# Two PSUM pools of a hybrid encoder block, opened in the other order

## The chip, the cores and the metric

The kernel runs on one core of a Trainium2 chip. The metric is the device time of one execution in microseconds (us), as the median of several runs. Before the change it is 1249.9 us, the median of three runs from 1248.79 to 1251.98. A difference of 0.3% (3.7 us) is about the least that a measurement of this kernel can tell from no change.

## What is computed

One layer of an encoder for 256 tokens of width 2048, all in float32:

```
n = RMSNorm(h)
[GDN inputs | HGRN2 inputs] = n @ W_in
y_A = gated DeltaNet group (8 heads of 128)
y_B = HGRN2 group (8 heads of 128: gate, chunkwise recurrence, gated RMSNorm)
h = h + concat(y_A, y_B) @ W_out
h = h + relu(RMSNorm(h) @ W1)^2 @ W2
out = RMSNorm(h)
```

The change concerns the border between the last two HGRN2 heads and the product with W_out, a 256 x 2048 by 2048 x 2048 product.

## The kernel before

**Products.** A float32 operand is split in two float32r parts, `hi` (a cast on ScalarE, ACT, line 120) and `lo` (a subtraction on VectorE, DVE, line 121). Weights come in tiles of 128 x 2048 floats (`w`, 1 MB, three buffers), which SyncE (SP) loads in order. Each tile is split in two halves of 1024 columns into three buffers of `hi` and three of `lo`. So the cast of one half has to wait until TensorE (PE) has read the half three before it.

**Stages.** The input projection and the sixteen heads ("mixers") are software-pipelined: while the weights of head n+1 are multiplied (lines 331, 332 and 358), head n is mixed. Heads 0 to 7 are GDN, heads 8 to 15 HGRN2. After the input projection's last matmul, the mixing of heads 14 and 15 is left. Then comes the output projection (line 845): two passes (`nh` = 0, 1) of 16 blocks `k`, one for each head's 128 columns of y. A block is 12 matmuls of 512 columns: 4 with `hi` and 2 with `lo` for each of two halves of the tokens. A pass adds into four banks: `acc` for the first pass and `accb` for the second. The MLP follows (lines 874 to 876).

**The end of a mixer** (`hgrn_mix`). Its matmuls come in three groups. The names are those of their tiles:

- `pd` and `pa` (lines 693 to 708): the scores in the chunks. DVE masks and adds them up (711, 715), POOL spreads them (718) and ACT copies the rest (721 to 725) into `A`.
- `poh` (727 to 729): the head's output from `A`. ACT and DVE norm it (479 to 483).
- `pt` (487): its transpose. ACT and DVE (491, 492) write it to `yTa` (heads 0 to 11) or `yTb` (heads 12 to 15), which the output projection reads: block k reads head k.

Ahead of `pd` stands a chain of small steps on ACT, DVE and POOL (lines 639 to 682).

**Banks.** PSUM has eight banks of 2 KB a partition, and each tile here is one. `psM` holds the mixers' four (two `mx`, two `sv`). `psP` holds the input projection's four: two `acc` of `project`, two `tok` of `project_tokens`, which `tokens_out` (line 367, ACT) reads last. Both pools close at `mctx.close()`. Then `psA` (the `acc` above) and `psB` (`accb`) open, with four banks each. A pool takes the lowest banks free, so before the change `psA` takes those of `psM` and `psB` those of `psP`:

```python
    mctx.close()
    psA = ctx.enter_context(tc.tile_pool(name="psA", bufs=4, space=PSUM))
    psB = ctx.enter_context(tc.tile_pool(name="psB", bufs=4, space=PSUM))
    ...
    for nh in range(2):
        acc = (acc_a, acc_b)[nh]
        accs = [acc() for _ in range(4)]
```

**Order.** Each engine works through its instructions in the order in which they stand. That order comes from a scheduler, which lays the instructions out by its own estimate of when each could run. A matmul into a bank that a pool has taken over waits for the last reader of what was there.

Of the kernel before, what the change touches and what calls it, by code (L numbers as in the profile page):

```python
# [12 lines left out]
PSUM = bass.MemoryType.PSUM  # L13
# [62 lines left out]
def hybrid_block(ctx: ExitStack, tc: tile.TileContext, x, xt, w_in, w_ab, params, w_out, w_ff1, w_ff2,  # L76
# [19 lines left out]
    yTa = ypool.tile([P, NYA, 2 * T], F32R, tag="yT", name="yTa")  # L96
    mctx = ExitStack()
    mp = mctx.enter_context(tc.tile_pool(name="mp", bufs=1))
    psM = mctx.enter_context(tc.tile_pool(name="psM", bufs=MXB, space=PSUM))
    psP = mctx.enter_context(tc.tile_pool(name="psP", bufs=2, space=PSUM))  # L100

    def wtile():
        return wpool.tile([P, 2048], F32, tag="w", name="w")
# [1079 lines left out]
```

## Time and profile before

| | |
|---|---|
| median of 3 runs | 1249.9 us |
| the profiled execution | 1249.3 us, of which its span 1247.6 us |
| PE busy | 97% of the span |
| DVE, ACT, POOL busy | 83%, 62%, 10% |
| weights read and the rest | 233.44 MB, 187 GB/s in the mean |
| granted PE clock | 0.985 in the mean |

Times in the profile are counted from the start of the span. A row of the timeline gives the start, the length, the engine, the line and the operation, with the tiles written and read. In square brackets stands how long the engine had been idle, and what ended that. A row of the windows gives for a stretch each engine's busy time with its count of instructions, and then the granted clock of PE, the DMA engines' busy share and GB/s. "PEld" is the loading of PE's stationary operand, which overlaps the matmuls.

### The profile page before, as it was taken

The numbers are of one execution on the slowest core, as the hardware profiler recorded it, in microseconds if no ns is written. First come the engines' busy times: TensorE is split into PE (matmuls) and PEld (weight loads), VectorE is DVE, ScalarE is ACT, GpSimd is POOL, SyncE is SP. The second block draws the span as 40 slices with busy tenths as digits, with TensorE's granted clock in tenths as the row PEclk, the third lists the DMA queues.
The fourth block names the chain that finished last, engine by engine and source line by source line (L and its number), as shares of the span: only waits on it lengthen the run. The fifth ranks groups of instructions, "written<-read, shape, count | busy, mean of one in ns | idle before, by whom it ended". The sixth has DMA issues, their size and how long they took to land.

```text
span 1247.6 us, 18180 instructions
## 1 busy us (share of the span) xinstructions
PE 1215.6 (97%) x6894; PEld 1013.8 (81%) x6894; DVE 1033.4 (83%) x1443; ACT 776.8 (62%) x1150; POOL 118.9 (10%) x177
## 2 busy tenths in 40 slices
PE   9999999997999959999999999999999999999997
PEld 7888888886888848888888888888888888888886
DVE  7888997786779854768898989898998888988887
ACT  7668666664768653646655656666666656656553
POOL 0132432153211110000000000000000000000000
PEclk9999999998999969999999999999999999999999
DMA  9456455552335525765465455554775555565461
GB/s 332 160 161 200 159 190 180 190 177 93 103 136 203 168 69 169 246 210 188 165 236 200 172 202 203 188 187 165 276 273 198 201 199 203 184 221 201 170 236 68
DMA packets 37143, 233.44 MB, mean 187 GB/s; under 512 B 4696, under 2 KB 5728, under 8 KB 10176
## 3 DMA queue, kind: packets, MB, share of 16 engines
q1 hardware_dynamic: 34848, 229.83, 52.7%
q0 software_dynamic: 1632, 1.72, 0.7%
q8 instruction: 54, 0.88, 0.3%
q10 hardware_dynamic: 576, 0.74, 0.2%
q14 instruction: 33, 0.27, 0.1%
HBM read 227.67 MB, written 4.60 MB: 186 GB/s over the span
## 4 chain that ended last, share of the span: by engine, by line
PE 92%; POOL 2%; issue 2%; DMA 2%; DVE 1%; ACT 1%; SPq 0%; POOLq 0%; DVEq 0%; ACTq 0%
PE acc L358 10%; PE acc L875 9%; PE acc L876 9%; PE acc L874 9%; PE accb L875 8%; PE accb L874 8%; PE accb L876 8%; PE acc L331 8%; PE acc L332 4%; PE acc L845 4%; PE accb L845 3%; PE accv L331 2%; PE accv L332 1%; POOL X L513 1%; PE acc L886 1%
## 5 line engine op out<-in xcount | busy, mean ns | idle before, releaser
L121 DVE TENSOR_TENSOR lo<-w,hi 128x1024 fp32r<-128x1024 f32 (+1 forms) x422 | 485.8, 1167 | 124.3 <-ACT hi L120 116.5
L120 ACT CAST hi<-w 128x1024 fp32r<-128x1024 f32 (+1 forms) x422 | 413.5, 993 | 240.7 <-PE acc L875 53.1
L331 PE MATMUL acc<-xT,hi 128*128 128x512 f32 x512 | 180.6, 399 | 1.7 <-ACT hi L120 1.7
L120 ACT CAST hi<-TT 128x1024 fp32r<-128x1024 f32 x88 | 92.0, 1052 | 77.9 <-issue 21.7
L332 PE MATMUL acc<-xT,lo 128*128 128x256 f32 x512 | 140.4, 285 | 0.0
L121 DVE TENSOR_TENSOR lo<-TT,hi 128x1024 fp32r<-128x1024 f32 x88 | 106.8, 1221 | 29.5 <-ACT hi L120 27.2
L358 PE MATMUL acc<-hi,xT 128*128 128x512 f32 x384 | 119.1, 398 | 0.0
L331 PEld LDWEIGHTS acc<-xT,hi 128*128 128x128 f32 x512 | 94.9, 189 | 21.6 <-ACT hi L120 2.2
L874 PE MATMUL acc<-hi,sets 128*128 128x512 f32 x260 | 101.4, 391 | 0.0
L875 PE MATMUL acc<-hi,sets 128*128 128x512 f32 x260 | 101.2, 390 | 0.0
L332 PEld LDWEIGHTS acc<-xT,lo 128*128 128x128 f32 x512 | 96.7, 190 | 4.5 <-DVE lo L121 1.2
L876 PE MATMUL acc<-lo,sets 128*128 128x512 f32 x260 | 95.9, 390 | 0.0
L874 PE MATMUL accb<-hi,sets 128*128 128x512 f32 x224 | 88.0, 393 | 0.0
L875 PE MATMUL accb<-hi,sets 128*128 128x512 f32 x224 | 87.3, 390 | 0.0
L358 PEld LDWEIGHTS acc<-hi,xT 128*128 128x128 f32 x384 | 71.9, 191 | 14.9
L876 PE MATMUL accb<-lo,sets 128*128 128x512 f32 x224 | 78.8, 392 | 0.0
L875 PE MATMUL acc<-hi,gs 128*128 128x512 f32 (+1 forms) x200 | 77.0, 385 | 0.0
L874 PE MATMUL acc<-hi,gs 128*128 128x512 f32 (+1 forms) x200 | 76.7, 385 | 0.0
L1014 POOL TENSOR_TENSOR fin<-fin,cst 128x1 f32<-128x1 f32 x2 | 1.1, 568 | 781.2 <-DVE fin L1013 781.2
L876 PE MATMUL acc<-lo,gs 128*128 128x512 f32 (+1 forms) x200 | 75.6, 385 | 0.0
L358 PE MATMUL acc<-lo,xT 128*128 128x512 f32 x192 | 73.5, 399 | 0.0
L875 PE MATMUL accb<-hi,gs 128*128 128x512 f32 x188 | 73.1, 389 | 0.0
(362 smaller groups left out, 2359.6 us busy)
## 6 DMA issues: line engine op xcount, KB each, us to landing
w<-in_w_ff_dram SPq DMA_DIRECT2D x128, 1024.0 KB, 5.0
w<-in_w_in_dram SPq DMA_DIRECT2D x61, 1024.0 KB, 5.0
w<-in_w_out_dram SPq DMA_DIRECT2D x16, 1024.0 KB, 5.0
w<-in_w_in_dram SPq DMA_DIRECT2D x12, 256.0 KB, 5.4
big<-in_xt_dram SPq DMA_DIRECT2D x8, 256.0 KB, 5.6
h<-in_x_dram SPq DMA_DIRECT2D x2, 1024.0 KB, 8.6
scr_h<-h SPq DMA_DIRECT2D x4, 512.0 KB, 7.3
tail<-scr_h SPq DMA_DIRECT2D x2, 1024.0 KB, 6.0
```

The source lines that it names most:

```text
L120: ACT.copy(hi, w)
L121: eng.tensor_tensor(out=lo, in0=w, in1=hi.bitcast(F32), op=ALU.subtract)
L331: PE.matmul(accs[g], lhsT=hi[:, kk, g, :], rhs=xT[:, k, :], start=(k == 0), stop=False)
L332: PE.matmul(accs[g][:, T:], lhsT=lo[:, kk, g, :], rhs=xT[:, k, 0:T], start=False, stop=(k == KT - 1))
L358: PE.matmul(accs[hf], lhsT=xT[:, k, a + hf * P:a + hf * P + P], rhs=ww[:, cs], start=(k == 0 and a == 0 and ww is hi), stop=(k == KT - 1 a ...
L513: POOL.tensor_tensor(out=X[:, j + 1:, 0:ncol], in0=X[:, j + 1:, 0:ncol], in1=t3, op=ALU.subtract)
L845: PE.matmul(accs[2 * hf + c], lhsT=st, rhs=ww[:, c * 512:(c + 1) * 512], start=(k == 0 and a == 0 and ww is hi), stop=(k == 2 * NH - 1 and ...
L874: PE.matmul(dst, lhsT=ah, rhs=bh, start=start, stop=False)
L875: PE.matmul(dst, lhsT=al, rhs=bh, start=False, stop=False)
L876: PE.matmul(dst, lhsT=ah, rhs=bl, start=False, stop=stop)
L886: PE.transpose(pt[:, c * P:(c + 1) * P], src[:, c * P:(c + 1) * P], ident)
L1014: POOL.tensor_tensor(out=r, in0=r, in1=C("nhalf"), op=ALU.pow)
```

## The change

`psP` is opened ahead of `psM`. So the lower four banks are now the input projection's, and `psA`, which the output projection's first pass adds into, takes those. `psB` takes the mixers'.

```diff
     mp = mctx.enter_context(tc.tile_pool(name="mp", bufs=1))
+    psP = mctx.enter_context(tc.tile_pool(name="psP", bufs=2, space=PSUM))
     psM = mctx.enter_context(tc.tile_pool(name="psM", bufs=MXB, space=PSUM))
-    psP = mctx.enter_context(tc.tile_pool(name="psP", bufs=2, space=PSUM))
```

No instruction is added or taken away. The order of POOL and SP stays as it was. That of PE, ACT and DVE is changed only between the end of the input projection and the end of the output projection's first pass.

On PE, right after the last `pa` matmul of head 14, there stood the rest of head 14 and the whole of head 15, and then the first pass (lines with a minus are before, lines with a plus are now):

```order
 L708 MATMUL pa<-L 128x128
-L727 MATMUL poh<-ig,A 128x128
-L728 MATMUL poh<-ig,A 128x128
-L729 MATMUL poh<-ig,A 128x128
-L487 MATMUL pt<-cst,ig 128x128 x2
-L693 MATMUL pd<-E 32x32 x32
-L696 MATMUL pd<-gx 32x64 x8
-L702 MATMUL pa<-E 32x32 x4
-L706 MATMUL pa<-E 64x64 x2
-L708 MATMUL pa<-L 128x128
```

Now the first pass follows that `pa` directly, and what is left of the two heads stands in it, at five places. The `poh` of head 14 comes after 38 matmuls of the pass (`acc`), in the middle of a block:

```order
-L845 MATMUL acc<-hi,yTa 128x512 x4
+L845 MATMUL acc<-hi,yTa 128x512 x2
+L727 MATMUL poh<-ig,A 128x128
+L728 MATMUL poh<-ig,A 128x128
+L729 MATMUL poh<-ig,A 128x128
+L845 MATMUL acc<-hi,yTa 128x512 x2
```

The `pt` of head 14 comes after 82 of the pass's 192 matmuls, with `pd` of head 15 behind it. `pa` of head 15 comes after 100, its `poh` after 122 and its `pt` after 149.

On ACT, the casts of the output projection's weights (`hi<-w`) stood behind the last step of head 15. Twelve of them now stand between the steps of heads 14 and 15; the first of those places is here, where `u`, `E` and `ec` belong to head 15, and `A` and `uz` to head 14 and the gates:

```order
 L217 ACTIVATE uz<-uz 128x512
+L120 CAST hi<-w 128x1024
 L654 ACTIVATE u<-u 128x2x256
 L722 COPY A<-pa 64x2x64
 L725 COPY A<-pa 32x2x32 x2
 L376 ACTIVATE uz<-uz 128x512
+L120 CAST hi<-w 128x1024
 L670 ACTIVATE E<-gx 128x256
```

So each of these steps now stands behind one cast more than before, and the casts themselves come earlier than the last steps of the mixers. The subtractions of the `lo` parts (line 121) move on DVE in the same way, twelve of them ahead of the last step of head 15.

## The prediction

> **What bounds the kernel now.** I read the page first: span and busy time.
>
> ```profile
> span 1247.6 us, 18180 instructions
> PE 1215.6 (97%) x6894; PEld 1013.8 (81%) x6894; DVE 1033.4 (83%) x1443; ACT 776.8 (62%) x1150; POOL 118.9 (10%) x177
> ```
>
> PE is the bound. It has 32 us without a matmul, and the question is where those lie and whether the change reaches them. So I next read the windows by stage: the border that the change moves, the two passes of the output projection, and the first and last of the five stretches of the MLP.
>
> ```profile
> 441.60:465.14 23.54, 10.54 (x199) 7.98 (x198) 13.90 (x33) 12.21 (x34) 4.75 (x7) 0.64 0.14 46
> 465.14:510.50 45.36, 45.36 (x193) 37.46 (x194) 21.48 (x19) 18.16 (x18) 0.00 (x0) 0.96 0.53 178
> 510.50:557.00 46.50, 46.50 (x214) 38.60 (x214) 31.86 (x43) 26.26 (x35) 0.00 (x0) 1.00 0.63 215
> 557.00:700.00 143.00, 143.00 (x664) 118.85 (x664) 125.92 (x150) 90.75 (x115) 0.00 (x0) 1.00 0.54 190
> 1150.00:1233.00 83.00, 83.00 (x368) 68.73 (x367) 69.99 (x88) 45.29 (x55) 0.00 (x0) 1.00 0.48 171
> ```
>
> The first row is the border: of 23.54 us PE is busy 10.54, the granted clock is 0.64 in the mean, and no other engine is full either (DVE 13.90, ACT 12.21, DMA share 0.14). This is a chain of small steps, not a lack of any engine. From 465.14 on PE is busy all the time until 1233. The list of PE's waits from 465 to the end has one entry, and that is the end of the border itself:
>
> ```profile
> PE acc L845 <- DVE yTb L492: 1.1, 1, 1.1
> ```
>
> So whatever is taken from the time before the second pass should reach the end whole: nothing behind it has slack of PE to swallow it. The timeline shows what the border consists of.
>
> ```profile
> 443.15 0.69 ACT L367 ACTIVATE ig<-acc,gnw 128x512 f32<-128x512 f32 x1
> 443.54 0.49 PE L708 MATMUL pa<-L 128*128 128x128 f32 x2
> 448.21 0.77 PE L727 MATMUL poh<-ig,A 128*128 128x128 f32 x2 [4.18 <-POOL u L655]
> 452.84 0.66 PE L487 MATMUL pt<-cst,ig 128*128 128x128 f32 x2 [3.01 <-DVE ig L483]
> 454.95 1.35 PE L693 MATMUL pd<-E 128*32 128x32 f32 x64 [1.45 <-DVE E L678]
> 459.83 0.76 PE L727 MATMUL poh<-ig,A 128*128 128x128 f32 x2 [1.20 <-POOL A L718]
> 463.40 0.66 PE L487 MATMUL pt<-cst,ig 128*128 128x128 f32 x2 [1.95 <-DVE ig L483]
> 465.14 2.08 PE L845 MATMUL acc<-hi,yTa 128*128 128x512 f32 x4 [1.08 <-DVE yTb L492]
> ```
>
> From 444.03 (443.54 + 0.49) PE waits in turn for POOL, DVE, DVE, POOL, DVE and DVE. The last row is the point: the first matmul of the output projection reads `yTa`, which has long been there, yet it starts only when DVE has written the last `yTb`, the last read of a mixers' bank. The banks hold it, not the data.
>
> **The change, part by part.** *The wait for banks.* The first pass now needs the projection's banks, whose last reader is ACT's line 367: 443.15 + 0.69 = 443.84. That is ahead of 444.03, where PE ends the `pa` of head 14, behind which the pass now stands. So the pass starts at 444.03 instead of 465.14. *What it takes there.* Its speed is read where PE runs it at full clock, from the chain that ended last:
>
> ```profile
> 465.14 45.34 PE acc L845 x192
> 499.83 10.65 PE acc L845 x47
> 510.49 4.31 PE accb L845 x19
> ```
>
> 10.65 / 47 = 0.2266 us a matmul, so 192 x 0.2266 = 43.5 us. Before it took 45.34, the difference being its start at half clock, which the windows of 2 us show:
>
> ```profile
> 446.00:448.00 2.00, 0.00 (x0) 0.00 (x0) 1.24 (x4) 1.08 (x4) 1.82 (x3) 1.00 0.01 4
> 448.00:450.00 2.00, 1.62 (x6) 1.35 (x6) 1.27 (x2) 1.48 (x6) 1.11 (x2) 0.50 0.00 0
> 470.00:472.00 2.00, 2.00 (x10) 1.67 (x9) 1.22 (x1) 0.34 (x2) 0.00 (x0) 1.00 0.00 0
> ```
>
> The clock was still 1.00 up to 448, though PE stood still in that row, and it was back at 1.00 by 470. So a pass that starts at 444.03 starts at full clock, and those 1.8 us go too.
>
> *The mixers' matmuls that stand in the pass.* `poh` and `pt` of head 14, all four groups of head 15. Their price at full clock is read from head 13's, which ran between the projection's matmuls:
>
> ```profile
> 416.96 0.63 PE L693 MATMUL pd<-E 128*32 128x32 f32 x50
> ...
> 418.27 0.49 PE L708 MATMUL pa<-L 128*128 128x128 f32 x2
> 426.60 0.38 PE L727 MATMUL poh<-ig,A 128*128 128x128 f32 x2
> ...
> 427.04 0.39 PE L729 MATMUL poh<-ig,A 128*128 128x128 f32 x2
> 436.46 0.38 PE L487 MATMUL pt<-cst,ig 128*128 128x128 f32 x2
> ```
>
> `pd` with `pa`: 416.96 to 418.76, 1.80 us. `poh`: 426.60 to 427.43, 0.83. `pt`: 0.38. Together 1.80 + 2 x 0.83 + 2 x 0.38 = 4.2 us. From start to start instead of start to end (the next matmul can begin some 0.2 us ahead of an end, as the pairs of rows above overlap) it would be about 3.3; I take 4.2 and keep 3.3 for the range.
>
> *The sum.* The second pass began at 510.49. Now: 444.03 + 43.5 + 4.2 = 491.7, if PE waits nowhere in between. That is 18.8 us less.
>
> *Does PE wait at the five places?* PE reaches each at 444.03 plus its count of matmuls x 0.2266 plus the groups ahead of it. When the data are there I worked out by walking each queue in its new order, with a cast at 1.055 and a subtraction at 1.225 us. Each cast also waits for PE to leave the buffer three blocks back.
>
> ```profile
> L120 ACT CAST hi<-w x19: 1036/1055/1057, 442.2 to 510.1; 128x1024 fp32r<-128x1024 f32 x19
> L121 DVE TENSOR_TENSOR lo<-w,hi x19: 1218/1225/1226, 440.5 to 508.4; 128x1024 fp32r<-128x1024 f32 x19
> 447.70 0.41 ACT L725 COPY A<-pa 32x64 f32<-32x64 f32 x2
> 452.35 0.60 DVE L483 SCALAR_TENSOR_TENSOR ig<-poh,ss,ig 128x128 f32<-128x128 f32 x2
> 452.52 1.48 ACT L669 ACTIVATE E<-E 128x1536 f32<-128x1536 f32 x1 [1.33 <-DVE E L663]
> 454.04 1.77 DVE L678 TENSOR_TENSOR E<-E,gx 128x256 f32<-128x256 f32 x5 [0.76 <-ACT E L669]
> 455.72 0.68 DVE L679 TENSOR_TENSOR E<-E,gx 128x512 f32<-128x512 f32 x1
> ```
>
> `poh` of head 14: `A` was there at 448.1 and is now one cast later, 449; PE comes at 444.03 + 38 x 0.2266 = 452.6. `pt` of head 14: `ig` was there at 452.95, and `poh` now runs 4.4 us later. On ACT it stands behind the exponential of head 15's `E` (line 669), which a cast and a subtraction more put at 454.0 to 455.5; then come the two squares to 456.4, a cast to 457.5 and the scale to 458.0. On DVE the two steps on `E` (678, 679) end at 458.1, a subtraction at 459.3, and `ig` at 459.9. PE comes at 444.03 + 82 x 0.2266 + 0.8 = 463.4. If instead the three casts and three subtractions between the two groups all came one after the other, it would be 452.95 + 4.4 + 3 x 1.055 + 3 x 1.225 = 464.2, 0.8 us too late. The other places by the same walk: `pd` of head 15: its inputs at 457.4, PE at 463.8. `pa`: 460.3 against 468.9. `poh` of head 15: its scores leave PE at about 469.9, and ACT's four copies end at 471.0; PE comes at 474.7. `pt` of head 15: 477.8 against 481.6. Block 15 needs head 15's `yTb`: 483.1 against 489.0. The smallest margin is 3.5 us, so I charge nothing; without it PE stands still by what is missing, once, since later places keep the margin that they had.
>
> *The casts themselves.* A block takes PE 12 x 0.2266 = 2.7 us, ACT 1.06 and DVE 1.23. Over the pass ACT has 12.2 us of the border and 18.2 of the pass (windows above) in 48, DVE 13.9 + 21.5. Neither is full. *DMA:* SP's order is unchanged. A tile's load is issued when its predecessor three tiles back is split, 16 us ahead of its use, in the order as before. *The second pass:* its banks are now the mixers', last read at 483.1, against a start at 491.7. Nothing is added there; its place in the order is the same.
>
> *A rule that speaks against the change.* POOL's steps of the chain vary much in this trace:
>
> ```profile
> L718 POOL TENSOR_TENSOR A<-rd,cst_a x16: 397/438/1114, 286.1 to 458.7; 128x128 f32<-128x128 f32 x16
> L658 POOL TENSOR_SCALAR gx<-gx x8: 854/1266/1672, 262.9 to 449.1; 128x256 f32<-128x256 f32 x8
> L655 POOL TENSOR_TENSOR u<-u x8: 721/740/1321, 257.8 to 447.5; 128x256 f32<-128x256 f32 x8
> ```
>
> At worst, from the shortest to the longest, head 15 pays 0.6 (L655) + 0.8 (L658) + 2 x 0.7 (L718) = 2.8 us. That is below the 3.5 of margin, so the sum stays. The Trainium skill ("SBUF — State Buffer", section "Who interferes with whom") says that a DVE instruction with two SBUF inputs contends with a GpSimd instruction that reads SBUF. The subtractions of line 121 are of that kind, and twelve now run beside POOL's steps; by that rule the longer ends of these rows would be the usual ones.
>
> **The rivals.** *Places that bind (12%).* The casts and the mixers hinder each other, so that PE is held. At the very worst all twelve casts and all twelve subtractions lie in series with the old chain: the last `pt` then comes at 463.40 + 12 x 1.055 + 12 x 1.225 = 490.8, and 43 matmuls follow it: 490.8 + 0.4 + 43 x 0.2266 = 500.9. The gain is then 9.6 us, the time 1249.3 - 9.6 = 1239.7. For it: ACT and DVE take their queues in order, and a cast that waits for PE holds up the mixer step behind it. Against it: the margins above. The same bound says that this alone can't make the kernel slower.
>
> *Given back later (4%).* The 18.8 us reappear as a wait of PE behind the pass, for instance because DVE, busy 125.92 of 143 us from 557 to 700, is late with what it must split. The time is then 1249.3. Against it: PE does not wait once there, and everything there is shifted together.
>
> *Slower: the clock (3%).* The border was a rest for PE, which would now work on to 1233 without one. If the granted clock then sank in the 723 us from the second pass to 1233, the gain is eaten from 18.8 / (723 + 18.8), a clock of 0.975. At 0.96, the mean of the first pass, the lowest of the busy rows above, it costs 723 x (1/0.96 - 1) = 30.1 us: 1249.3 - 18.8 + 30.1 = 1260.6. Against it: 676 us of unbroken work at 1.00 in the rows from 557 to 1233.
>
> *The change doesn't do it (1%).* If `psA` still waited for a mixers' bank: 1249.3. The new order, in which mixers' matmuls stand inside the pass, could not run at all then.
>
> **How the numbers follow.** The profiled execution took 1249.3 us, its span and 1.7 us around it; 1249.3 - 18.8 = 1230.5. The median of the runs is 0.6 higher, which gives 1231.1; I say 1231.0. That case has 80%. The low end: inserts at 3.3 instead of 4.2 give 1229.6, and the fastest of the runs was 1.1 below the median: 1228.5. The high end goes into the first rival, to 1237.5, two thirds of the way to its worst; beyond it lie about 4% of that rival and the 8% of the others, below the low end a few per cent. A measurement of this kernel can tell about 0.3%, 3.7 us, from no change. The forecast and the first rival are both faster than that: 92%. Same: 5%, slower: 3%.
>
> **What would show it.** In the profile after, the first L845 matmul starts near 444 behind ACT's L367, the first `accb` near 492, and the granted clock between them is 1.00 throughout. PE's list of waits loses its entries at `poh` and `pt` of heads 14 and 15. POOL's three lines show whether they are longer than before, and by less than 3 us together. It is wrong if PE idles at `poh` or `pt` inside the pass (the first rival, by as much), if a wait of PE shows up behind 492, or if the clock's row for the MLP is below 1.00.

## The result, and the profile after

The changed kernel takes 1230.15 us, the median of four runs (1228.59 to 1234.20), against 1249.43 for the kernel before beside it. The ratio is 0.985, with an interval from 0.982 to 0.987: 1.3 to 1.8% faster. The profiled execution took 1230.33 us.

The page after, in the same lines as before:

```profile
span 1228.5 us, 18177 instructions
PE 1210.9 (99%) x6894; PEld 1009.7 (82%) x6894; DVE 1032.5 (84%) x1443; ACT 776.0 (63%) x1150; POOL 119.8 (10%) x177
```

PE is busy 4.7 us less than it was (1210.9 against 1215.6 us), in a span that is 19 us shorter. The windows show where: the border and the first pass, the start of the second pass, and two of the MLP's stretches.

```profile
441.60:492.00 50.40, 50.40 (x349) 41.55 (x337) 35.95 (x52) 29.88 (x52) 5.48 (x7) 1.00 0.56 193
492.00:538.50 46.50, 46.50 (x215) 38.64 (x214) 31.91 (x42) 26.30 (x36) 0.00 (x0) 1.00 0.63 211
700.00:850.00 150.00, 149.44 (x689) 123.55 (x688) 130.01 (x145) 90.29 (x112) 0.00 (x0) 1.00 0.55 193
1130.00:1215.00 85.00, 85.00 (x377) 70.38 (x376) 71.55 (x90) 47.12 (x59) 0.00 (x0) 1.00 0.48 172
```

Border and first pass are one stretch now, with PE busy all through it at a granted clock of 1.00. What PE waits for behind 445 is this, the whole list:

```profile
PE acc L886 <- ACT C L978: 0.4, 1, 0.4
PE accb L876 <- DVE lo L121: 0.2, 1, 0.2
```

The waits at `poh` and `pt` of heads 14 and 15 are gone. Two small ones in the MLP are new, 0.6 us together. They are not the change's: the run with `psB` first (below), whose border is the same, has neither, and the run of the kernel before with extra matmuls has both. The timeline has the first matmul of the pass, the mixers' groups in it, and the start of the second pass. No row has a bracket, so PE never stood still ahead of one.

```profile
441.95 0.69 ACT L367 ACTIVATE ig<-acc,gnw 128x512 f32<-128x512 f32 x1
442.34 0.49 PE L708 MATMUL pa<-L 128*128 128x128 f32 x2
442.69 1.19 PE L845 MATMUL acc<-hi,yTa 128*128 128x512 f32 x4
451.44 0.38 PE L727 MATMUL poh<-ig,A 128*128 128x128 f32 x2
462.12 0.38 PE L487 MATMUL pt<-cst,ig 128*128 128x128 f32 x2
473.66 0.38 PE L727 MATMUL poh<-ig,A 128*128 128x128 f32 x2
480.48 0.38 PE L487 MATMUL pt<-cst,ig 128*128 128x128 f32 x2
490.50 1.75 PE L845 MATMUL accb<-hi,yTa 128*128 128x512 f32 x7
```

From head 14's last `pa` (442.34) to the second pass (490.50) it is 48.16 us. Before, the same stretch ran from 443.54 to 510.32, 66.78 us. The difference, 18.6 us, is the change's work. The rest of the 19.0 between the two profiled executions is made of two parts that have nothing to do with it: the stretch began 1.2 us earlier, and what follows it took 0.85 us longer (739.83 against 738.98 to the end of the execution).

That stretch, called the border below, is the measure that the experiments are compared by, beside their times: it does not contain a scatter of some 5 us that the profiled executions show at a place far ahead of it (last section).

### The profile page after: what moved, and what is told of

The parts are those of the page before. It is cut to its first block, busy times and chain, and to the rows that moved or that the text cites. A ratio compares the mean times of both kernels' runs of the same rounds, so it can differ in the third digit from the quotient of the medians.

```text
span 1228.5 us, 18177 instructions
## 1 busy us (share of the span) xinstructions
PE 1210.9 (99%) x6894; PEld 1009.7 (82%) x6894; DVE 1032.5 (84%) x1443; ACT 776.0 (63%) x1150; POOL 119.8 (10%) x177
## 4 chain that ended last, share of the span: by engine, by line
PE 93%; DMA 2%; POOL 2%; DVE 1%; issue 1%; ACT 0%; SPq 0%; POOLq 0%; DVEq 0%
PE acc L358 10%; PE acc L874 9%; PE acc L876 9%; PE acc L875 9%; PE acc L331 8%; PE accb L876 8%; PE accb L875 8%; PE accb L874 8%; PE acc L332 4%; PE acc L845 4%; PE accb L845 4%; PE accv L331 2%; PE accv L332 1%; POOL X L513 1%; DMA w<-in_w_ff_dram 1%
```

## The experiments

Each is told with its edit. Three theories stand against each other. Early start: the gain is PE's idle time at the border, filled because the first pass no longer waits for the mixers' last read of a bank. Placement: it matters which banks the projection and the mixers lie in. Clock: the gain is mainly PE's clock staying up.

### Which pool inherits which banks

The kernel before, with `psB` opened ahead of `psA`:

```diff
-    psA = ctx.enter_context(tc.tile_pool(name="psA", bufs=4, space=PSUM))
     psB = ctx.enter_context(tc.tile_pool(name="psB", bufs=4, space=PSUM))
+    psA = ctx.enter_context(tc.tile_pool(name="psA", bufs=4, space=PSUM))
```

> The kernel before with psP and psM opened in the old order, but psB opened ahead of psA at the end, so that the first pass again inherits the projection's banks, now the upper four. All engines' orders are those of the change. Early start (the gain is PE's idle time at the border, filled because the pass no longer waits for the mixers' last read of a bank): 1230 us, 1227 to 1234, first acc matmul near 443. Placement (the gain comes from which banks the projection and the mixers lie in, which are those of before here): 1249 us.

It took 1233.5 us, ratio 0.986 (0.984 to 0.988). Its border is 48.16 us (447.27 to 495.43), to the hundredth that of the change. Its start is some 5 us later in the profile, from the scatter ahead of it.

The same edit in the changed kernel:

> The change, and psB opened ahead of psA as well, so that the first pass inherits the mixers' banks again while the projection and the mixers lie where the change put them. All engines' orders are those of before. Early start: 1249.5 us, 1247 to 1252, first acc matmul near 464. Placement: 1230 us.

1248.6 us, ratio 0.999 (0.998 to 1.001), border 66.77 us (442.30 to 509.07), that of before. So placement falls: banks of either half give either time. What counts is only whether the first pass inherits from the pool whose last reader is early. In the border's traces the instructions of PE, ACT and DVE stand in the first of these runs in the order of the change, and in the second in that of the kernel before. So in these four kernels the early banks and the order that the scheduler makes with them come together; no run has the early banks with the old order.

### The data instead of the banks

The changed kernel, with the weight tile of heads 14 and 15 taken first in the first pass (the start and stop flags go with it):

```diff
-        for kp in range(8):
+        for kp in ((7, 0, 1, 2, 3, 4, 5, 6) if nh == 0 else range(8)):
```

> The change, with the first pass taking its weight tiles in the order 7, 0, 1, 2, 3, 4, 5, 6, so that its first two blocks read heads 14 and 15. The banks are free early as in the change, but the data are not. Early start: only block 14 (12 matmuls) can fill the border, and block 15 waits for the old chain, so most of the gain goes: 1247 us, 1244 to 1249.5. If the banks or the casts' earlier places alone made the gain: 1230 us.

1245.8 us, ratio 0.996 (0.994 to 0.997). The banks are free, and 16 of the 18.6 us are gone: the border is 63.90 us (446.94 to 510.84). The list of PE's waits in it, from 440 to 511, names the chain again. (`poh` reads `A` and not `u`: the row names the step that ended last, and ACT's last copy into `A` ended 0.07 us ahead of it.)

```profile
PE pt L487 <- DVE ig L483: 5.0, 2, 3.0
PE poh L727 <- POOL u L655: 4.3, 1, 4.3
PE acc L846 <- ACT yTb L491: 1.5, 2, 0.9
```

The same tile as the fourth, `(0, 1, 2, 7, 3, 4, 5, 6)`:

> The change, with the first pass taking its weight tiles in the order 0, 1, 2, 7, 3, 4, 5, 6: 72 matmuls stand ahead of the blocks of heads 14 and 15 instead of 168. Early start: PE comes to the last pt and to block 15 some 3 to 4 us too early and waits there: 1234 us, 1231.5 to 1237. If the border's chain were hidden wherever the blocks stand: 1230 us. If the casts stretched the chain as far as in the first rival on record: 1240 us or more.

1233.1 us, ratio 0.987 (0.985 to 0.990), border 51.30 us (442.12 to 493.42), 3.1 us more than with the change. In the timeline PE is seen to come too early to the last `pt` and to block 15:

```profile
467.74 0.50 PE L487 MATMUL pt<-cst,ig 128*128 128x128 f32 x2 [1.95 <-DVE ig L483]
468.80 1.66 PE L846 MATMUL acc<-hi,yTb 128*128 128x512 f32 x6 [0.56 <-ACT yTb L491]
```

So an early start is worth as much as there are matmuls that don't need the late data: 12 of them are worth 2.9 us of border, 72 are worth 15.5, 168 all of it.

### A longer chain

Eight more POOL steps in head 15's chain, in the kernel before. They multiply by 1, so the values stay as they are:

```diff
         POOL.tensor_scalar(pb[:, 0, :], b, -1.0, None, ALU.mult)
+        for _ in range(8 if hd == NH - 1 else 0):
+            POOL.tensor_scalar(pb[:, 0, :], pb[:, 0, :], 1.0, None, ALU.mult)
```

> The kernel before with eight more POOL steps in head 15's chain (each multiplies the negated cumulative sum by 1, some 1.15 us, 9.2 us together). Early start: the chain sets the border's length in the kernel before, so the steps cost all of it: 1258.6 us, 1256 to 1261. If PE's work or the clock set the border's length: well under 1255 us.

1259.2 us, ratio 1.0073 (1.0049 to 1.0096). The border is 74.95 us (440.84 to 515.79), 8.2 more than before. The steps took 7.4 us here, 0.9 each and not the 1.15 expected, and PE's wait for the same chain shows them: its longest is now

```profile
PE pd L695 <- DVE E L680: 10.0, 1, 10.0
```

Of the 8.2, 0.9 lie in the first pass itself, which took 46.11 us at a clock of 0.94, where it took 45.2 at 0.96 before; the other 7.2 are the chain's. In the kernel before, then, the chain sets the border, and a delay in it costs its full length. That the time came out so near the 1258.6 expected is in part luck, since the steps were shorter than assumed, and the ten runs spread from 1254.35 (the profiled one) to 1263.50. The same eight steps in the changed kernel:

> The change with the same eight POOL steps, 9.2 us. Early start: the chain runs beside the first pass, whose block 15 has some 6 us to spare, so about 3 us of the 9.2 show: 1233 us, 1229.5 to 1236. If the chain still sets the end (places that bind): 1239 us.

1228.2 us, ratio 0.981 (0.978 to 0.985), border 47.86 us (441.86 to 489.72). The 9.6 us that the steps take here cost nothing at all, and the time lies below the expected range. I had taken the 6 us ahead of block 15 for all that there is to spare. But PE lets data lie ahead of each mixers' group, and the scheduler, which knows of the steps, put head 15's `pd` later, at 467.93 instead of 462.43.

Sixteen and 24 steps, to find where the cover ends:

> The change with 16 of the extra POOL steps in head 15's chain, 19.2 us at the 1.2 us that each took. In the run with 8 they ended at 459.45 of the profile and cost nothing; now they should end near 469. From that step to the last write of yTb the border before took 14.9 us, and casts may add up to 6: 484 to 490, where block 15 begins at about 487. Early start: 0 to 3 us lost, 1231 us, 1228 to 1235. If nothing of the chain were hidden beyond the first 9 us: 1239 us.

> The change with 24 of the extra POOL steps, 28.7 us, which end near 478.5. By the same sum the last yTb comes at 493.5 to 499.5, so that PE waits 6 to 12 us for it at the end of the first pass: 1239 us, 1235 to 1243. If the first pass could hide any chain: 1229 us. If the steps cost in full from the ninth on: 1248 us.

With 16: 1230.6 us, ratio 0.984 (0.982 to 0.986), border 49.38 us (442.01 to 491.39), 1.2 more than with the change. With 24: 1241.2 us, ratio 0.993 (0.990 to 0.995), border 58.88 us (443.41 to 502.29), 10.7 more. In the timeline of the second of these PE waits at the last groups as it did in the kernel before:

```profile
489.00 0.49 PE L710 MATMUL pa<-L 128*128 128x128 f32 x2 [0.96 <-DVE L L684]
492.78 0.76 PE L729 MATMUL poh<-ig,A 128*128 128x128 f32 x2 [3.29 <-POOL A L720]
496.30 0.66 PE L487 MATMUL pt<-cst,ig 128*128 128x128 f32 x2 [1.90 <-DVE ig L483]
497.52 2.93 PE L847 MATMUL acc<-hi,yTb 128*128 128x512 f32 x6 [0.56 <-ACT yTb L491]
```

The chain is hidden up to some 18 us of extra length and shows nearly in full beyond that: from 16 steps to 24 the steps' time grows by 10.9 us (18.96 to 29.84) and the border by 9.5. In these two runs as well the scheduler moved head 15's groups back (its last `pa` stands at 477.65 and 489.00, against 468.30 in the change). So the 18 us hold for an order made with the steps known, not for the change's own order with a chain that turns out late; that was not run. Nor do POOL's steps test the first rival on record, that the casts hinder the chain. Against that one stands the change's own trace, where PE waits at none of the five places.

### The clock alone

The kernel before with 16 extra float32 matmuls in the border, which read the chain's own tiles as they come and write a bank of the projection that nothing reads (the other calls of `busy` stand behind line 658, ahead of the tile `ec`, and around `poh`):

```diff
+        keep = acc_p("acc") if hd == NH - 1 else None
+
+        def busy(n, src):
+            for _ in range(n if hd == NH - 1 else 0):
+                PE.matmul(keep[:, 0:T], lhsT=ident, rhs=src, start=True, stop=True)
+        busy(5, KQ[:, 1, :])
```

> The kernel before with 16 extra float32 matmuls of 256 columns put into the border, into a bank of the projection that nothing reads, so that PE's clock stays up; everything waits as before. Early start: the clock's share is at most 1.8 us in the pass and some 4 in the mixers' groups at half clock, less what the extra matmuls hold up: 1246 us, 1243 to 1250. If the gain were mainly the clock: 1232 to 1236 us.

1247.7 us, ratio 0.999 (0.997 to 1.001): within the interval no difference. Its windows, border and first pass:

```profile
446.90:468.97 22.07, 13.96 (x143) 10.71 (x142) 12.58 (x31) 9.87 (x31) 4.90 (x7) 0.92 0.09 36
468.97:512.63 43.66, 43.65 (x192) 36.16 (x193) 21.04 (x18) 17.97 (x18) 0.00 (x0) 1.00 0.53 180
```

The clock stayed up (0.92 and 1.00 against 0.64 and 0.96), and the pass took 43.66 us where it took 45.2 before (465.14 to 510.32). The 1.5 us are the clock's share of it, 1.8 in the prediction. But the stretch ahead of the pass, from `pa` on, took 22.54 us (446.44 to 468.98) where it took 21.60 before (443.54 to 465.14), so the extra matmuls held the chain up by more than a faster PE took from it. The whole border, 66.19 us (446.44 to 512.63), is 0.6 less than before. What the clock would bring without that hindrance isn't told apart here. The clock as the main cause falls: with PE near full clock the waits for the chain are still there. It has a share in the change's gain all the same, which the sum in the next section shows.

## Why the prediction was right, point by point

*What bounds the kernel.* Held. The border was a chain of waits and no lack of any engine: what lengthens the chain lengthens the border by as much in the kernel before.

*The wait for banks.* The pass was to start right behind `pa` of head 14, with ACT's line 367 out of the way. It started 0.35 us after `pa`'s start and 0.05 after the end of line 367 (442.64). In the profile that is at 442.69 and not near 444, since all before it ran 1.2 us earlier.

*The sum.* From the start of `pa` to the second pass I had 491.7 - 443.54 = 48.2 us; it is 48.16, or 48.3 by the chain's own start of the second pass, 490.66. That chain shows the terms, the matmuls of the pass in their pieces between the mixers' groups (starts, lengths, counts):

```profile
442.82 8.78 PE acc L845 x38
452.27 10.01 PE acc L845 x44
463.42 4.32 PE acc L845 x18
468.78 5.04 PE acc L845 x22
474.49 6.16 PE acc L845 x27
480.87 9.80 PE acc L845 x43
```

The pieces add up to 44.11 us for 192, 0.2297 each, against 43.5. The gaps between them, the mixers' groups, are 0.67, 0.22 + 0.92 (to 463.42), 1.04, 0.67 and 0.22: 3.7 us, between the 4.2 that I took and the 3.3 of the other reading. The two errors nearly cancel, so that the sum is right to some 0.1 us is luck; the terms are off by 0.6 and 0.5.

The same terms show what the 18.6 us are made of. PE's six waits in the border before, the brackets in the prediction's timeline, add up to 12.9 us. The mixers' groups took the rest of 444.03 to 465.14, 8.2 us, and take 3.7 now: 4.5 us less. The pass went from 45.34 to 44.11: 1.2 us less. So about two thirds of the gain are PE's idle time. Most of the other third is its clock, which was 0.50 in the windows of 2 us from 448 to 468 before and is 1.00 now: head 13's groups at full clock were worth 4.2 us. In the change PE stands still nowhere in the border and the clock stayed up, so this third came along with the early start and isn't a rival to it.

*The five places.* Held, and close. Where the walk through the queues had `ig` of head 14 at 459.9 and PE at 463.4, a margin of 3.5 us, DVE's row and PE's after give 458.59 and 462.12:

```profile
446.93 0.41 ACT L725 COPY A<-pa 32x64 f32<-32x64 f32 x2
456.25 0.68 DVE L679 TENSOR_TENSOR E<-E,gx 128x512 f32<-128x512 f32 x1
457.99 0.60 DVE L483 SCALAR_TENSOR_TENSOR ig<-poh,ss,ig 128x128 f32<-128x128 f32 x2
458.51 0.41 DVE L682 TENSOR_TENSOR L<-E,ec 128x256 f32<-128x256 f32 x1
469.14 0.42 ACT L725 COPY A<-pa 32x64 f32<-32x64 f32 x2
475.89 0.61 DVE L483 SCALAR_TENSOR_TENSOR ig<-poh,ss,ig 128x128 f32<-128x128 f32 x2 [0.59 <-ACT ss L481]
481.41 0.48 DVE L492 SCALAR_TENSOR_TENSOR yTb<-pt,gnw,yTb 128x256 fp32r<-128x256 f32 x1
```

The last `yTb` ends at 481.89, where I had 483.1, all of it 1.2 us earlier by the start. The other rows show the last step ahead of `poh` of head 14 (PE at 451.44), `pd` (462.43), `pa` (467.67), `poh` (473.66) and `pt` (480.48) of head 15. The data are there 4.0 to 8.8 us ahead of PE, and all the walk's times, taken 1.2 us earlier, hold within 0.8 us. The bounds from casts and subtractions all in series were far too wide: they put the last `pt` at 490.8, and it ran at 480.48 without a wait.

*POOL's steps.* The rows after show the stretch that was to be looked for. In the border, all but the first are head 15's:

```profile
444.98 1.32 POOL L718 TENSOR_TENSOR A<-rd,cst_a 128x128 f32<-128x128 f32 x2 [12.60 <-DVE rd L715]
446.95 1.25 POOL L655 TENSOR_TENSOR u<-u 128x256 f32<-128x256 f32 x1 [0.65 <-ACT u L654]
449.09 1.14 POOL L658 TENSOR_SCALAR gx<-gx 128x256 f32<-128x256 f32 x1 [0.88 <-DVE gx L657]
450.31 1.02 POOL L667 TENSOR_TENSOR E<-gx 128x256 f32<-128x256 f32 x1
466.02 0.76 POOL L718 TENSOR_TENSOR A<-rd,cst_a 128x128 f32<-128x128 f32 x2 [14.70 <-DVE rd L715]
```

Line 655 took 1.25 us beside DVE's subtraction from 446.38, where it took 0.72 at 447.46 before, and line 667 took 1.02 for 0.85. The others took what they took before. That is 0.7 us together, within the 2.8 allowed for, and it was hidden.

*Given back later.* Not seen: the 0.6 us of new waits in the MLP come and go without the change. *The clock.* It stayed at 1.00 in all windows from the border to 1215, so the slower rival did not come about.

## What to carry to other kernels

When one stage's accumulators take over banks, ask who reads the old contents last, and let the next stage inherit from the pool whose last reader is early; which banks they are made no difference here. The gain is bounded by the work of the next stage that doesn't need the late data: count the matmuls that can stand ahead of them, and walk each queue once in the new order to see that nothing comes late at the places where the old stage's steps now stand. Here that walk was right to within 0.8 us.

## What I had not expected of the hardware

*One POOL step takes 7.73 us in some executions.* It is the first multiplication of the inversion (line 511), 128 x 15 elements. The rows are of the run with `psB` first and of the change:

```profile
268.56 7.73 POOL L511 TENSOR_TENSOR Xt<-X 128x15 f32<-128x15 f32 x1
```

```profile
267.69 0.90 POOL L511 TENSOR_TENSOR Xt<-X 128x15 f32<-128x15 f32 x1
```

Of eleven profiled executions of these kernels it took 7.73 us in three, and from 0.21 to 0.90 in the others. In those three PE's `poh` of head 8 waits 7.4 to 7.6 us for POOL instead of about 2.6 to 3.1, and the border starts at 446.4 to 447.3 instead of 440.8 to 443.5. That fits the scatter of some 5 us in the times of most kernels here (1228.59 to 1234.20 for the change), but only profiled executions show it, and the times of two kernels (8 and 16 steps in the change) spread by less than 2 us. What makes the step long was not tried.

*POOL slows beside DVE.* The same added POOL step, 128 x 256 elements, took 851 ns each of eight times in the kernel before, while no subtraction of line 121 ran, and up to 1701 in the changed one, while four did:

```profile
L660 POOL TENSOR_SCALAR gx<-gx x8: 851/851/851, 447.6 to 454.1; 128x256 f32<-128x256 f32 x8
```

```profile
L660 POOL TENSOR_SCALAR gx<-gx x8: 851/1050/1701, 449.9 to 457.7; 128x256 f32<-128x256 f32 x8
```

Line 121 reads `w` and `hi`, and the added step reads and writes one tile, all in SBUF. The Trainium skill ("SBUF — State Buffer", section "Who interferes with whom") says that a DVE instruction with two SBUF inputs contends with a GpSimd instruction that reads SBUF. These rows agree: together it is 9.6 us against 7.4, so some 0.55 us for each subtraction beside it, by estimate.
